# Weights split once and kept as parts in DRAM, the mixer's gates first, the output stage in idle buffers

## The chip, the cores and the metric

The kernel runs on one core of a Trainium2 chip. The metric is the device time of one execution in microseconds (us); lower is better. TensorE (PE) does the matmuls, VectorE (DVE), ScalarE (ACT) and GpSimd (POOL) the elementwise work, and every DMA is issued by SyncE (SP), whose queue works in order.

## The reference

One decoder block over 2048 tokens of width 1024, in float32:

```
h      = rmsnorm(x, norm_g) * (1 + scale) + shift        # scale, shift, gate from c @ w_ada + b_ada
q,k,v, z_attn, u, z_pool, g_attn, g_pool = split(h @ w_in)
attn   = three groups of dilated window attention, joined by a softmax over their log-denominators
y_attn = (attn * silu(z_attn)) @ w_attn_br
pooled = trailing mean of u over 2, 4, 8 or 16 tokens (one window a group of 128 channels), minus u
mixed  = pooled @ pool_w (per group) * pool_scale
y_pool = (mixed * silu(z_pool)) @ w_pool_br
merged = sigmoid(g_attn) * y_attn + sigmoid(g_pool) * y_pool
out    = rmsnorm(x + gate * (merged @ w_out), final_g)
```

## The kernel before

**Halves and products.** The tokens are worked in two halves of 1024 (h = 0, 1). Every large operand is held as two float32r parts, high and low; a product is three matmuls, high x high, high x low and low x high (`mm3`, L255: one k-step is six matmuls of 512 columns; one projection of 128 columns is eight k-steps into the PSUM tile `mm`).

**The weights.** They lie packed in DRAM as 80 blocks of 512 KB (`stream`, `pack_weights`). The stream `order` runs over all 80, then again over the last 8 (`w_out`, used once per quarter), and all that twice, so 176 blocks are fetched. `fetch_raw` (L203) loads a block into `wraw` (two buffers), and `fetch_part` splits a half block into the tiles `whi` (a DVE cast, L217) and `wlo` (a POOL subtraction, L218). There are six of each, so parts are made up to six ahead. A part's buffer is refilled two `tick`s after the k-step that read it last. Each `fetch_raw` is placed in SP's queue right behind the split that frees its buffer.

**The order of work.** PE and SP keep the order in which the program is written; DVE, ACT and POOL are ordered by a planner. Each half does twelve units (four head pairs, three groups each: `unit` projects k, q, v), while the attention of the unit before is woven in as a side queue. In a unit of the last group, `load_rows` (L639) fetches the other groups' results from DRAM, `output` joins them on DVE (L756 to L773), and `joined` transposes the result on PE (L777). Then come:

- `pool_in`: four projections of u, with the attention of the last unit woven in; after each, `pool_sums` queues the running sums of that group on DVE (L879 to L896);
- `pool_out`: four projections of z_pool, each followed by sigmoid, the group's small matmuls (L926) and a split into `gated`;
- `branch` (pool), `attn_gate`, `branch` (attention), where each of eight turns multiplies a gate's projection by a product with `gated`;
- `out_half` twice (quarters q = 0, 1): `merged @ w_out` (L1003, 32 steps of twelve 256-column matmuls), `finish` adds the product to `y` (rows of x loaded again, L276), and `normed` scales a row tile into a new tile `yo` and stores it.

In half 0, `ahead` and `next_h` run beside the two `out_half`s and prepare half 1: eight tiles of x are loaded (`new_x`, L276), normed (`x_norm`, L293 to L295), transposed on PE two tiles at a time (`transposed_x`, L340; eight steps a pair of tiles) and split into `hparts` (L345 to L348). In `next_h`, tiles 4 to 7 are loaded after the pass over a pair ends, and normed in steps 3 and 4 of the next pass.

**Buffers.** Most [128 x 1024] tiles come from one pool of `NBIG` = 33 slots (`b4`): `hparts` (16 slots), `gated`, `merged`, the splits of `merged`, x, `y`, `yo`, `yt`, and the two rows `gate` and `fg` among them. A tile waits for a slot to come free, and a DMA that waits for one holds SP's queue.

Of the kernel before, what the change touches and what calls it, by code (L numbers as in the profile page):

```python
# [11 lines left out]
F32 = mybir.dt.float32  # L12
# [134 lines left out]
def block_kernel(ctx: ExitStack, tc: tile.TileContext, x, cols, b_gate, w_ada, wpk, pool_w, rel_bias, final_g, onehot,  # L147
# [38 lines left out]
    def mm():  # L186
        return ps_mm.tile([P, HALF], F32, name="mm", tag="mm")
# [97 lines left out]
    def new_x(h, p):  # L285
        xt = b4(name="x")
        load_x(h, p, xt)
        return xt
# [540 lines left out]

    def branch(hparts, gated, merged, mparts=None):  # L830

# [3 lines left out]
        for u in range(4):  # L835
# [3 lines left out]
            for j in range(2):  # L839
                ps = mm()  # L840
                yield from mm3(ps, take("col"), hparts)
                sg = sigmoid(ps)
# [5 lines left out]
                ps = mm()  # L848
                yield from mm3(ps, wb, gated, slice(j * P, (j + 1) * P), frees=(j == 1))
                msl = slice(j * 512, j * 512 + 512)  # L850
# [10 lines left out]

    def pool_in(h, hparts, pooled, todo):

        for gi in range(4):
            ps = mm()
            for _ in mm3(ps, take("col"), hparts):
                next(todo[0], None) if todo else None
                yield
            cur = b4(name="u0")
            nc.scalar.copy(out=cur, in_=ps)  # L870
            todo[:] = [chain(*todo, pool_sums(h, gi, cur, pooled))]

    def pool_sums(h, gi, u0, pooled):
# [24 lines left out]
        phi, plo = b4(F32R, "phi"), b4(F32R, "plo")  # L898
        split(phi, plo, cur)
        pooled.append((phi, plo))  # L900
        yield

    def pool_weights():
# [5 lines left out]
        return pwh, pwl  # L909

    def pool_out(hparts, pooled, gated, pwh, pwl, todo):
        for gi in range(4):
            ps = mm()
            for _ in mm3(ps, take("col"), hparts):
                next(todo[0], None)
                yield
            assert len(pooled) > gi
            sg = sigmoid(ps)
            nc.vector.tensor_tensor(out=sg, in0=ps, in1=sg, op=ALU.mult)
            phi, plo = pooled[gi]  # L920
            gsl = slice(gi * P, (gi + 1) * P)
            for q in range(2):
                sl = slice(q * 512, (q + 1) * 512)
                ps = bank(q)
                for i, (w, m) in enumerate(((pwh, phi), (pwh, plo), (pwl, phi))):
                    nc.tensor.matmul(ps, lhsT=w[:, gsl], rhs=m[:, sl], start=(i == 0), stop=(i == 2))  # L926
                nc.vector.scalar_tensor_tensor(out=sg[:, sl], in0=ps, scalar=psc_col[:, gi:gi + 1], in1=sg[:, sl],
                                               op0=ALU.mult, op1=ALU.mult)
            ghi, glo = b4(F32R, "gphi"), b4(F32R, "gplo")
            split(ghi, glo, sg)  # L930
            gated.append((ghi, glo))

# [35 lines left out]
    def out_half(h, q, mparts, rows_bc):  # L968
# [16 lines left out]
        def normed(p):  # L985
            y = ys[p]
            ssq = sm.tile([P, 1], F32, name="ssq")
            nc.vector.tensor_reduce(out=ssq, in_=ssqs[p], axis=AX.X, op=ALU.add)
            r = rstd(ssq, nc.gpsimd)
            yo = b4(name="yo")  # L990
            nc.vector.tensor_tensor(out=yo, in0=y, in1=fg_bc, op=ALU.mult)
            nc.scalar.activation(out=yo, in_=yo, func=AF.Copy, scale=r)
            t0 = h * HALF + (4 * q + p) * P
            store(out[t0:t0 + P, :], yo, 2)

        for n in range(4):
# [9 lines left out]
            if n < 3:  # L1006

                for k in range(KC):
# [32 lines left out]
    for h in range(2):  # L1041
# [3 lines left out]
        for hp in range(4):  # L1045
            for g in GORDER:
# [12 lines left out]
                n_queue = 7 if g else 8  # L1059
        pooled, merged, gated = [], [], []  # L1060
        pwh, pwl = pool_weights()
        todo = []
        weave(pool_in(h, hparts, pooled, todo), 32, queue, n_queue, 1)
        run(queue)
# [8 lines left out]
        nc.sync.dma_start(out=rows_bc[1], in_=final_g.partition_broadcast(P))  # L1073
        mparts = []
# [61 lines left out]
```

## Time and profile before

| | |
|---|---|
| median of 3 runs | 2218.45 us (2213.07 to 2219.28) |
| profiled execution | 2212.21 us, of which the span from first to last instruction is 2210.2 us |
| PE busy | 2137.7 us (97% of the span) |
| DVE, ACT, POOL busy | 933.1, 597.6, 805.9 us |
| DMA | 198.48 MB, mean 90 GB/s |
| mean granted TensorE clock | 0.989 |

Busy times overlap; the engine with the longest is PE. A wait of PE is a stretch in which it had nothing running, put down to the instruction that ended it.

### The profile page before, as it was taken

The page shows a single profiled execution, that of the slowest core. Times are in us where ns is not written, and L with a number is a line of the kernel's source. Part 1 is how long each engine was busy: PE and PEld are TensorE (multiplying, and loading weights), DVE is VectorE, ACT ScalarE, POOL GpSimd, SP SyncE. Part 2 cuts the span into 40 slices and gives each one's busy share as a digit, 9 for nine tenths or more (in the row PEclk, how much of TensorE's full clock was granted, in tenths as well). Part 3 has the DMA queues.
Part 4 walks back from the last instruction along what each step waited for, and adds up shares of the span by engine and source line. Part 5 has one row for each costly group of instructions (what it writes and reads, how often), then busy time and mean ns, then how long its engine had stood idle before and what let it go on. Part 6 is the DMA issues. An engine that isn't in the chain of part 4 may idle for free.

```text
span 2210.2 us, 30824 instructions
## 1 busy us (share of the span) xinstructions
PE 2137.7 (97%) x11786; PEld 1808.5 (82%) x11786; DVE 933.1 (42%) x2144; ACT 597.6 (27%) x1487; POOL 805.9 (36%) x669
## 2 busy tenths in 40 slices
PE   6999999999999999999799999999999999999998
PEld 4888888888878888889778878888888788888898
DVE  6536335263382111117743464553644831111164
ACT  4423333233321001003433333333333310010023
POOL 3313222132243225437743232332333432253375
PEclk9999999999999999999999999999999999999999
DMA  8442232222211112114432333223222111121134
GB/s 294 142 153 73 81 95 73 73 74 80 76 60 42 48 48 87 52 43 172 162 120 87 89 90 89 72 82 111 81 81 86 53 48 48 48 86 48 48 134 162
DMA packets 142675, 198.48 MB, mean 90 GB/s; under 512 B 13542, under 2 KB 109983, under 8 KB 142528
## 3 DMA queue, kind: packets, MB, share of 16 engines
q1 hardware_dynamic: 142528, 196.51, 27.9%
q8 instruction: 93, 1.52, 0.3%
q14 instruction: 54, 0.44, 0.1%
HBM read 157.62 MB, written 35.16 MB: 87 GB/s over the span
## 4 chain that ended last, share of the span: by engine, by line
PE 42%; DVE 3%; DMA 2%; issue 2%; POOL 2%; ACT 1%; SPq 0%; POOLq 0%; DVEq 0%; ACTq 0%
PE mm L255 33%; PE mm L1003 3%; PE knot L738 3%; PE qk L682 2%; DMA row<-rows 1%; POOL wlo L218 1%; PE knot L717 1%; PE knot L646 1%; ACT l L692 1%; DMA wraw<-in_wpk_dram 1%; DVE wd L762 0%; DVE l L701 0%; DVE whi L217 0%; PE hp L926 0%; POOL y L982 0%
## 5 line engine op out<-in xcount | busy, mean ns | idle before, releaser
L218 POOL TENSOR_TENSOR wlo<-wraw,whi 128x512 fp32r<-128x512 f32 x352 | 476.4, 1357 | 995.9 <-DVE whi L217 549.6
L255 PE MATMUL mm<-hhi,whi 128*128 128x512 f32 x2000 | 637.8, 400 | 0.0
L255 PE MATMUL mm<-hlo,whi 128*128 128x512 f32 x2000 | 621.4, 392 | 0.0
L255 PE MATMUL mm<-hhi,wlo 128*128 128x512 f32 x2000 | 619.5, 391 | 0.0
L217 DVE CAST whi<-wraw 128x512 fp32r<-128x512 f32 x349 | 189.6, 547 | 754.0 <-PE mm L255 628.7
L255 PEld LDWEIGHTS mm<-hhi,wlo 128*128 128x128 f32 x2000 | 377.4, 189 | 81.8
L255 PEld LDWEIGHTS mm<-hlo,whi 128*128 128x128 f32 x2000 | 377.1, 189 | 81.4
L255 PEld LDWEIGHTS mm<-hhi,whi 128*128 128x128 f32 x2000 | 364.7, 189 | 72.0 <-issue 0.5
L820 ACT ACTIVATE sg<-mm 128x1024 f32<-128x1024 f32 x48 | 49.4, 1028 | 555.1 <-PE mm L255 443.2
L686 DVE CUSTOM_DVE_ANT_0 l<-qk,bias 128x256 f32<-128x256 f32 (+1 forms) x384 | 126.0, 384 | 129.2 <-PE qk L682 105.9
L692 ACT ACTIVATE l<-l,row 128x256 f32<-128x256 f32 (+1 forms) x256 | 117.2, 460 | 149.0 <-DVE row L686 126.7
L1003 PE MATMUL mm<-whi,mhi 128*128 128x256 f32 x512 | 149.2, 291 | 1.0 <-DVE yt L1032 0.7
L1003 PE MATMUL mm<-whi,mlo 128*128 128x256 f32 x512 | 146.2, 286 | 2.5 <-POOL mlo L827 2.5
L1003 PE MATMUL mm<-wlo,mhi 128*128 128x256 f32 x512 | 145.9, 285 | 0.0
L738 PE MATMUL knot<-v,pT 128*128 128x64 f32 x768 | 131.5, 270 | 3.2 <-ACT pT L727 2.9
L738 PEld LDWEIGHTS knot<-v,pT 128*128 128x128 f32 x768 | 112.7, 193 | 5.7 <-ACT pT L727 3.2
L702 POOL TENSOR_TENSOR l<-l,ident 128x512 f32<-128x512 f32 (+1 forms) x56 | 71.6, 1278 | 108.5 <-DVE l L701 97.7
L738 PE MATMUL knot<-vd,pT 128*128 128x64 f32 x560 | 109.6, 278 | 1.3 <-DVE wd L762 1.3
L1003 PEld LDWEIGHTS mm<-whi,mlo 128*128 128x128 f32 x512 | 99.2, 194 | 3.3 <-POOL mlo L827 3.3
L1003 PEld LDWEIGHTS mm<-whi,mhi 128*128 128x128 f32 x512 | 99.5, 194 | 1.9 <-DVE yt L1032 1.5
L1003 PEld LDWEIGHTS mm<-wlo,mhi 128*128 128x128 f32 x512 | 99.5, 194 | 0.1
L727 ACT COPY pT<-knot 128x512 f32<-128x512 f32 x96 | 56.4, 588 | 155.1 <-PE knot L738 67.7
(175 smaller groups left out, 2497.3 us busy)
## 6 DMA issues: line engine op xcount, KB each, us to landing
wraw<-in_wpk_dram SPq DMA_DIRECT2D x176, 512.0 KB, 3.7
rows<-row SPq DMA_DIRECT2D x128, 66.0 KB, 1.7
row<-rows SPq DMA_DIRECT2D x64, 132.0 KB, 3.4
wada<-in_w_ada_dram SPq DMA_DIRECT2D x32, 256.0 KB, 5.5
x<-in_x_dram SPq DMA_DIRECT2D x16, 512.0 KB, 6.3
y<-in_x_dram SPq DMA_DIRECT2D x16, 512.0 KB, 7.7
out_dram<-yo SPq DMA_DIRECT2D x16, 512.0 KB, 6.5
khist<-kh SPq DMA_DIRECT2D x52, 128.0 KB, 2.5
```

The costliest lines, as they stand in the source:

```text
L217: copy(out=hi, in_=raw)
L218: nc.gpsimd.tensor_tensor(out=lo, in0=raw, in1=hi.bitcast(F32), op=ALU.subtract)
L255: nc.tensor.matmul(ps[:, n * 512:(n + 1) * 512], lhsT=w, rhs=m[:, n * 512:(n + 1) * 512], start=(k == 0 and j == 0), stop=(k == nk - 1 and ...
L646: nc.tensor.transpose(ps[:, (t % 4) * P:(t % 4) * P + P], res["vT"][:, k0:k0 + P], ident)
L682: nc.tensor.matmul(qks[i][:, j * 256:j * 256 + nk], lhsT=qt[qi][a], rhs=keys[ki][a], start=(n == 0), stop=(n == 2))
L686: nc.vector.tensor_tensor_reduce(out=l[:, 2 * j + i, 256 - nk:], in0=qks[i][:, j * 256:j * 256 + nk], in1=bt[:, i, 256 - nk:], scale=-1.0, ...
L692: nc.scalar.activation(out=ll, in_=ll, func=AF.Exp, scale=-1.0, bias=nd[:, j, i:i + 1], accum_out=nd[:, j, 2 + i:3 + i])
L702: nc.gpsimd.tensor_tensor(out=prev, in0=prev, in1=ident.unsqueeze(1).broadcast_to([P, 4 - f, P]), op=ALU.mult)
L727: nc.scalar.copy(out=pT[:, 1], in_=pps)
L738: nc.tensor.matmul(ops[:, j, hs], lhsT=d["pT"][:, b, 2 * j + i, :], rhs=vv[:, hs], start=(b == 1), stop=(b == 0 or not full))
L820: nc.scalar.activation(out=s, in_=ps, func=AF.Sigmoid)
L1003: nc.tensor.matmul(pst[:, pos:pos + 256], lhsT=st, rhs=mv, start=(fresh and i == 0), stop=(last and i == 2))
```

## The change

1. **Parts in DRAM.** When a block is split for the first time, both parts of each half block are also stored to a DRAM tile `wsp` (three ticks later). From the second time on, a half block is two 256 KB loads into `whi` and `wlo`, with no cast, no subtraction and no `wraw`.
2. **Mixer's gates first.** `pool_gates` (the z_pool projections) now runs where `pool_in` ran, beside the last attention. `pool_mix` then projects u, the groups in the order 3, 2, 1, 0; each group's sums, small matmuls and split (`pool_group`) are advanced one step per k-step of the projections that follow, those of the first turn of `branch` included. In that turn, the product with `gated` takes the groups in the order 3 to 0. Group 0 does its two subtractions on DVE.
3. **Output stage.** `gate`, `fg` (in two halves) and `yt` move from the 33 slots into attention tiles that are idle then (`pT`, `bias`, `l`); `yo` is gone, `y` is scaled in place.
4. **next_h.** Tiles of x are loaded at step 3 of the pass over an earlier pair, and normed in steps 4 and 5 of the next pass.

```diff
-    seq += [("in", OFF_U + c * P, "col") for c in range(4)]
     seq += [("in", OFF_ZP + c * P, "col") for c in range(4)]
+    seq += [("in", OFF_U + c * P, "col") for c in range(3, -1, -1)]
...
+    wsp = dram.tile([n_blocks, 2, 2, P, 512], F32, name="wsp")
...
-        if i < len(order):
+        if i < n_blocks:
             t = b4(name="wraw") if i == 2 else wp.tile([P, HALF], F32, name="wraw", tag="wraw", bufs=2)
...
         b, q = divmod(i, 2)
+        if b >= n_blocks:
+            hi = wp.tile([P, 512], F32R, name="whi", tag="whi", bufs=6)
+            lo = wp.tile([P, 512], F32R, name="wlo", tag="wlo", bufs=6)
+            for j, t in enumerate((hi, lo)):
+                nc.sync.dma_start(out=t.bitcast(F32), in_=wsp[order[b], q, j])
+            parts[i] = (hi, lo)
+            state["part"] = i + 1
+            return
...
         nc.gpsimd.tensor_tensor(out=lo, in0=raw, in1=hi.bitcast(F32), op=ALU.subtract)
+        for j, t in enumerate((hi, lo)):
+            store(wsp[b, q, j], t.bitcast(F32), 3)
...
-                if p and p < 6 and i in (3, 4):
-                    x_norm(tiles[p + i - 1])
+                if p and p < 6 and i in (4, 5):
+                    x_norm(tiles[p + i - 2])
+                if p < 4 and i == 3:
+                    tiles += [new_x(1, p + 4), new_x(1, p + 5)]
                 yield
-            if p < 4:
-                tiles += [new_x(1, p + 4), new_x(1, p + 5)]
...
+                for _ in mm3(ps, take("col"), hparts):
+                    advance(todo)
+                    yield
+                run(*todo)
...
+                turn = -1 if todo and not (u or j) else 1
+                yield from mm3(ps, wb[::turn], gated[::turn], slice(j * P, (j + 1) * P), frees=(j == 1))
...
+    def pool_gates(hparts, sgs):
+        for gi in range(4):
+            ps = mm()
+            yield from mm3(ps, take("col"), hparts)
+            sg = sigmoid(ps)
+            nc.vector.tensor_tensor(out=sg, in0=ps, in1=sg, op=ALU.mult)
+            sgs.append(sg)
+    def pool_mix(h, hparts, sgs, gated, pwh, pwl, todo):
+        gated += [None] * 4
+        for gi in range(3, -1, -1):
+            ps = mm()
+            for _ in mm3(ps, take("col"), hparts):
+                advance(todo)
+                yield
+            cur = b4(name="u0")
+            nc.scalar.copy(out=cur, in_=ps)
+            todo.append(pool_group(h, gi, cur, sgs, gated, pwh, pwl))
+    def pool_group(h, gi, u0, sgs, gated, pwh, pwl):
+        pooled, n = [], 0
+        for _ in pool_sums(h, gi, u0, pooled):
+            n += 1
+            yield
+        for _ in range((7, 8, 10, 11)[gi] - n):
+            yield
...
+        split(ghi, glo, sg, nc.gpsimd if gi else nc.vector)
+        gated[gi] = ghi, glo
...
-            yo = b4(name="yo")
-            nc.vector.tensor_tensor(out=yo, in0=y, in1=fg_bc, op=ALU.mult)
-            nc.scalar.activation(out=yo, in_=yo, func=AF.Copy, scale=r)
+            for i in range(2):
+                sl = slice(i * 512, (i + 1) * 512)
+                nc.vector.tensor_tensor(out=y[:, sl], in0=y[:, sl], in1=fg_bc[i], op=ALU.mult)
+            nc.scalar.activation(out=y, in_=y, func=AF.Copy, scale=r)
...
-                t = b4(name="yt").rearrange("p (t c) -> p t c", c=256)
+                t = att.tile([P, 4, 256], F32, name="yt", tag="l", bufs=2)
...
-        weave(pool_in(h, hparts, pooled, todo), 32, queue, n_queue, 1)
+        weave(pool_gates(hparts, sgs), 32, queue, n_queue, 1)
         run(queue)
-        run(pool_out(hparts, pooled, gated, pwh, pwl, todo))
-        run(branch(hparts, gated, merged))
+        todo = []
+        run(pool_mix(h, hparts, sgs, gated, pwh, pwl, todo))
+        run(branch(hparts, gated, merged, todo=todo))
...
-        rows_bc = b4(name="gate"), b4(name="fg")
+        rows_bc = (att.tile([P, D], F32, name="gate", tag="pT", bufs=1),
+                   [att.tile([P, 512], F32, name="fg", tag="bias", bufs=2) for _ in range(2)])
```

## Rows read from the trace of the kernel before

**Rows 1.** The page: busy time, share of the span and instructions of each engine.

```profile
PE 2137.7 (97%) x11786; PEld 1808.5 (82%) x11786; DVE 933.1 (42%) x2144; ACT 597.6 (27%) x1487; POOL 805.9 (36%) x669
```

**Rows 2.** Windows: stretch, length, busy us per engine (xcount), granted clock, DMA share, GB/s.

```profile
600.00:650.00 50.00, 45.52 (x242) 37.83 (x241) 46.56 (x101) 15.21 (x41) 24.82 (x15) 0.93 0.12 40
700.00:800.00 100.00, 100.00 (x443) 82.81 (x442) 16.71 (x31) 6.20 (x7) 25.64 (x20) 1.00 0.15 48
1001.00:1048.00 47.00, 45.17 (x370) 44.36 (x369) 36.25 (x37) 14.28 (x37) 37.79 (x32) 1.00 0.52 182
1060.00:1072.00 12.00, 10.35 (x88) 10.14 (x88) 10.23 (x16) 5.23 (x9) 8.93 (x10) 1.00 0.97 380
1722.00:1756.00 34.00, 29.03 (x145) 24.65 (x144) 32.62 (x67) 10.51 (x25) 14.85 (x9) 0.90 0.14 46
```

**Rows 3.** PE's waits, 1040 to 1120 us: us in total, times, longest.

```profile
PE hp L340 <- DVE x L295: 16.6, 3, 8.0
PE hp L340 <- ACT hraw L345: 1.7, 1, 1.7
```

**Rows 4.** Chain of work that ended last, 1085 to 1120 us: start, us, what.

```profile
1093.53 2.56 PE mm L1003 x12
...
1099.71 0.22 PE knot L340 x2
1099.92 1.43 PE mm L1003 x12
...
1106.45 4.05 DMA x<-in_x_dram
```

**Rows 5.** SP's waits, 1040 to 1120 us.

```profile
SPq L276 <- PE knot L340: 19.7, 2, 15.9
SPq L276 <- ACT yt L983: 6.5, 2, 3.7
```

**Rows 6.** PE's waits by stretch, in the order 100:600, 1125:1720, 600:660, 1700:1760, 2100:2210.

```profile
PE knot L777 <- DVE row L773: 5.5, 3, 2.0
...
PE knot L777 <- DVE row L773: 7.0, 3, 3.6
...
PE knot L777 <- DVE row L773: 3.2, 3, 2.2
PE knot L738 <- DVE wd L762: 1.3, 1, 1.3
...
PE knot L738 <- ACT pT L727: 2.9, 1, 2.9
PE knot L777 <- DVE row L773: 2.1, 2, 1.7
...
PE mm L1003 <- POOL mlo L827: 1.3, 2, 1.0
```

**Rows 7.** Timeline, 1284 to 1295 us: start, us, engine line op names.

```profile
1284.75 0.42 DVE L217 CAST whi<-wraw 128x512 fp32r<-128x512 f32 x1
...
1286.29 1.60 POOL L218 TENSOR_TENSOR wlo<-wraw,whi 128x512 fp32r<-128x512 f32 x1
...
1287.92 0.34 SPq L203 DMA_DIRECT2D wraw<-in_wpk_dram  x1
...
1288.43 0.79 SPq L639 DMA_DIRECT2D row<-rows  x2
...
1293.92 0.17 DVE L756 TENSOR_REDUCE mn<-row 128x4 f32<-128x12 f32 x1 [2.94 <-DMA row<-rows]
```

**Rows 8.** The page, costliest groups: line, engine, names, xcount, busy us, mean ns.

```profile
L218 POOL TENSOR_TENSOR wlo<-wraw,whi 128x512 fp32r<-128x512 f32 x352 | 476.4, 1357 | 995.9 <-DVE whi L217 549.6
```

**Rows 9.** DMA issues: xcount, KB each, median us to landing.

```profile
wraw<-in_wpk_dram SPq DMA_DIRECT2D x176, 512.0 KB, 3.7
...
x<-in_x_dram SPq DMA_DIRECT2D x16, 512.0 KB, 6.3
...
bias<-btab SPq DMA_DIRECT2D x24, 256.0 KB, 3.0
```

More of the change, by code (lines that the diff above doesn't have):

```diff
@@ L828, in msplit, with branch @@
         return [(hi[:, j * 512:(j + 1) * 512], lo[:, j * 512:(j + 1) * 512]) for j in range(2)]
-    def branch(hparts, gated, merged, mparts=None):
+    def branch(hparts, gated, merged, mparts=None, todo=()):
         add = bool(merged)
@@ L840, in branch @@
                 ps = mm()
-                yield from mm3(ps, take("col"), hparts)
+                for _ in mm3(ps, take("col"), hparts):
+                    advance(todo)
+                    yield
+                run(*todo)
                 sg = sigmoid(ps)
@@ L848, in branch @@
                 ps = mm()
-                yield from mm3(ps, wb, gated, slice(j * P, (j + 1) * P), frees=(j == 1))
+                turn = -1 if todo and not (u or j) else 1
+                yield from mm3(ps, wb[::turn], gated[::turn], slice(j * P, (j + 1) * P), frees=(j == 1))
                 msl = slice(j * 512, j * 512 + 512)
@@ L860, in branch @@
             mparts += msplit(merged[0][3])
-    def pool_in(h, hparts, pooled, todo):
+    def pool_gates(hparts, sgs):
         for gi in range(4):
             ps = mm()
+            yield from mm3(ps, take("col"), hparts)
[6 more added lines that the diff above has]
+            ps = mm()
             for _ in mm3(ps, take("col"), hparts):
-                next(todo[0], None) if todo else None
+                advance(todo)
                 yield
@@ L870, in pool_in, with advance @@
             nc.scalar.copy(out=cur, in_=ps)
-            todo[:] = [chain(*todo, pool_sums(h, gi, cur, pooled))]
+            todo.append(pool_group(h, gi, cur, sgs, gated, pwh, pwl))
+    def advance(gens):
+        for i in gens:
+            next(i, None)
+    def pool_group(h, gi, u0, sgs, gated, pwh, pwl):
[5 more added lines that the diff above has]
+            yield
+        sg = sgs[gi]
+        phi, plo = pooled[0]
+        gsl = slice(gi * P, (gi + 1) * P)
+        for q in range(2):
+            sl = slice(q * 512, (q + 1) * 512)
+            ps = bank(q)
+            for i, (w, m) in enumerate(((pwh, phi), (pwh, plo), (pwl, phi))):
+                nc.tensor.matmul(ps, lhsT=w[:, gsl], rhs=m[:, sl], start=(i == 0), stop=(i == 2))
+            nc.vector.scalar_tensor_tensor(out=sg[:, sl], in0=ps, scalar=psc_col[:, gi:gi + 1], in1=sg[:, sl],
+                                           op0=ALU.mult, op1=ALU.mult)
+        ghi, glo = b4(F32R, "gphi"), b4(F32R, "gplo")
+        split(ghi, glo, sg, nc.gpsimd if gi else nc.vector)
+        gated[gi] = ghi, glo
     def pool_sums(h, gi, u0, pooled):
@@ L898, in pool_sums @@
         phi, plo = b4(F32R, "phi"), b4(F32R, "plo")
-        split(phi, plo, cur)
+        split(phi, plo, cur, nc.gpsimd if gi else nc.vector)
         pooled.append((phi, plo))
@@ L909, in pool_weights @@
         return pwh, pwl
[L911 to L931, printed above, removed]
     def attn_gate(h, hparts, gated):
@@ L989, in normed @@
             r = rstd(ssq, nc.gpsimd)
-            yo = b4(name="yo")
-            nc.vector.tensor_tensor(out=yo, in0=y, in1=fg_bc, op=ALU.mult)
-            nc.scalar.activation(out=yo, in_=yo, func=AF.Copy, scale=r)
+            for i in range(2):
+                sl = slice(i * 512, (i + 1) * 512)
+                nc.vector.tensor_tensor(out=y[:, sl], in0=y[:, sl], in1=fg_bc[i], op=ALU.mult)
+            nc.scalar.activation(out=y, in_=y, func=AF.Copy, scale=r)
             t0 = h * HALF + (4 * q + p) * P
-            store(out[t0:t0 + P, :], yo, 2)
+            store(out[t0:t0 + P, :], y, 2)
         for n in range(4):
@@ L1059, in block_kernel @@
                 n_queue = 7 if g else 8
-        pooled, merged, gated = [], [], []
+        merged, gated, sgs = [], [], []
         pwh, pwl = pool_weights()
+        weave(pool_gates(hparts, sgs), 32, queue, n_queue, 1)
+        run(queue)
         todo = []
-        weave(pool_in(h, hparts, pooled, todo), 32, queue, n_queue, 1)
-        run(queue)
-        run(pool_out(hparts, pooled, gated, pwh, pwl, todo))
-        run(branch(hparts, gated, merged))
+        run(pool_mix(h, hparts, sgs, gated, pwh, pwl, todo))
+        run(branch(hparts, gated, merged, todo=todo))
         gated = []
@@ L1070, in block_kernel @@
         run(branch(hparts, gated, merged, m0))
-        rows_bc = b4(name="gate"), b4(name="fg")
+        rows_bc = (att.tile([P, D], F32, name="gate", tag="pT", bufs=1),
+                   [att.tile([P, 512], F32, name="fg", tag="bias", bufs=2) for _ in range(2)])
         nc.sync.dma_start(out=rows_bc[0], in_=gate_d)
-        nc.sync.dma_start(out=rows_bc[1], in_=final_g.partition_broadcast(P))
+        for i in range(2):
+            nc.sync.dma_start(out=rows_bc[1][i], in_=final_g[i * 512:(i + 1) * 512].partition_broadcast(P))
         mparts = []
```

## The prediction

> **What bounds the kernel now.** I read the page first: PE is busy for 97% of the span [rows 1]. In the windows the middle of a half has PE busy 100.00 of 100.00 us with 443 matmuls of 512 columns, one every 226 ns, at a granted clock of 1.00 [rows 2]. The change takes no matmul away, so nothing can be won there: all it can give back is PE's waits and the slow clock after them. The span holds about 72 us without a matmul (2210.2 - 2137.7), and PE's waits by stretch say where those lie that the change can reach: the end of half 0, the joins of the attention units, the change from attention to pooling, and a little in the first `out_half` of half 1 [rows 3, 6]. The chain and SP's waits then say what is late in each. The sum is a sum over those places.
>
> **Half 0's last quarter.** Between 1040 and 1120 us PE waits 16.6 us for normed tiles of x and 1.7 us for `hraw` [rows 3]. After such a wait, twelve matmuls that otherwise take 1.43 us take 2.56 us: the clock stands at the lower of its two levels, 1.2 instead of 2.4 GHz [rows 4]. That is 1.1 us for the twelve and some more before and after them, 1.5 us by my estimate, twice. In all some 21 us. What is late: SP waited 19.7 us in two waits for a transposed tile's slot and 6.5 us for a slot of `yt`, with the load of x at the head of its queue [rows 5]; the last tile was loaded at 1106.45 and PE needed it at about 1108 [rows 4]. Counting slots in the second pass: 16 of `hparts`, 8 of the split `merged`, 4 of `y`, 2 rows, 1 `yt` are 31 of 33, which leaves two for x, where tiles 2 and 3 are still being transposed; tiles 4 and 5 have no place. After the change the rows and `yt` are elsewhere: 28 are taken, five are left for x, so tiles 2, 3, 4, 5 and one more fit. A step of this stage takes 1.43 + 0.22 = 1.65 us [rows 4]. A load now comes nine steps (15 us) ahead of its norm instead of four (6.6 us), against 6.3 us to landing [rows 9]. Only tile 7 lacks a slot until step 15, when tiles 2 and 3 are done; its norm is at step 21, still 10 us on. On the other side, `y` itself is now held until its store has landed, and the seventh and eighth pair of `hparts` need those slots: I leave 4 us of waits for that. Gain 17 us; bounds 5 (the slots are short again) and 21.
>
> **The joins of half 1.** In the units of half 1 PE waits three times for the joined rows, 7.0 us in all [rows 6]. The longest one in the timeline: the cast `whi` is issued at 1284.75, `wlo` waits for POOL and ends at 1287.89, and only then SP issues the next `wraw` and behind it, at 1288.43, the two loads of rows, which land at 1293.9, behind 512 KB of weights [rows 7]. After the change there is no `wlo` and no `wraw` in half 1: the fetch waits for PE alone, which had released the cast, so the loads of rows go out about 3 us earlier, behind 0.8 us for issuing two part loads. I take 6 of the 7.0 us, and one stretch of low clock after the longest wait (about 1.5 us, as above) with it: 7 us; bounds 2 and 8.5.
>
> **From attention to pooling.** Half 0 waits 3.2 + 1.3 = 4.5 us there, half 1 2.9 + 2.1 = 5.0 us [rows 6], and the windows show why: DVE is busy 46.56 of 50 us and 32.62 of 34 us, because the running sums compete with the last attention [rows 2]. The granted clock in them is 0.93 and 0.90 [rows 2], which takes 0.07 x 50 = 3.5 us and 0.10 x 34 = 3.4 us at most, part of it while PE waits anyway: 2.5 us each. So 14.5 us. `pool_gates` leaves DVE four products there instead of the sums; the sums get 44 us of projections and the first 11 us of `branch` for themselves. What stays is the join that other units have, about 2 us a half. What is late next: group 0's `gated`. Its small matmuls end the projection; a DVE product, an ACT copy and a DVE subtraction follow, some 3.5 us by the like instructions (0.7, 1.0, 1.2 and the hand-overs), and PE reaches it as the fourth k-step, 3 x 6 x 0.226 = 4.1 us later. It fits by half a microsecond; I put 0.5 us a half on it (bounds 0 and 4, if DVE has something else in front). Gain 9 us; bounds 3 and 14.
>
> **In the first quarter of half 1** PE waits 1.3 us for POOL's `mlo`, which shares POOL with `wlo` [rows 6]; with 192 subtractions of 1357 ns less in the stream [rows 8], it goes: 1 us.
>
> **What is added.** 160 half blocks give 320 stores of 256 KB, all but the last few in half 0, and from then on 384 loads of 256 KB replace 96 of 512 KB: some 84 MB written and 50 MB more read. In the attention of half 0 they come between the loads of rows in SP's order. Two stores ahead of a load of rows cost it two issues (0.8 us, as the two in [rows 7]) and the time of 512 KB at the 380 GB/s that a window reached [rows 2], 1.4 us. The joins there wait 5.5 us already [rows 6]; those at the head now are behind a `wraw`, not where the stores come, so I take 2 us of loss (bounds 0 and 9: four joins by 2.2 us). The three-tick delay means a store never waits for its data. In the first quarter of half 0 the traffic is 47 us x 182 GB/s = 8.6 MB [rows 2]; ten half blocks are stored (5.2 MB) and six more are already loaded as parts (3.1 MB), less five `wraw` (2.6 MB): 14.3 MB in 47 us is 304 GB/s, below the 380 GB/s of the window at 1060 [rows 2]. It is hidden, with 80% of the queue full: loss 1 us, bounds 0 and 5. The store in place and the two halves of `fg` change nothing that PE waits for; after the last matmul the same DVE and ACT work remains.
>
> One limit is less clear. A 512 KB weight load lands in 3.7 us, a 256 KB one (`bias`) in 3.0 us [rows 9], so halving a DMA saves little of its time; that several run at once is seen only from the 380 GB/s, 2.7 times what one 512 KB load reaches by itself. The Trainium skill (DMA: Bandwidth & Descriptors, Anatomy of one DMA and Bandwidth) has the same shape: 2.0 us fixed plus the bytes, and the advice to make DMAs of 1 MiB or more. By its figures a part's two loads would take 5.2 us one after the other, 2.3 us more than PE's 2.9 us with a part of `w_out`, or 37 us a quarter; no run so far shows 256 KB loads queued like that. Where they did not is a rival below.
>
> **The sum.** 17 + 7 + 9 + 1 - 2 - 1 = 31 us off the profiled execution's 2212.2 us: 2181 us. The runs' median lies 6.2 us above the profiled execution; with that, 2187 us.
>
> **The rivals.**
>
> *The last quarter keeps its waits.* With `y` held until it lands and six tiles of x wanted at once, the slots are short again, and SP stands at a load of x as before (15.9 us, [rows 5]). Now no `wraw` is ahead: behind SP's wait stand the part loads, five parts of two steps (3.3 us) ahead, 16.5 us less 3 to 5 us of landing. A 15.9 us wait then costs PE 3 to 5 us for weights besides, so of the 17 us some 3 to 5 remain. Against it: three slots are really freed. Time: 2187 + 13 = 2200 us.
>
> *Half 0 pays.* Stores and rows collide at every join, with the clock falling after each (9 + 4 x 1.5 = 15 us), and the joins of half 1 keep half their waits (3 us). Together with the forecast's other terms 2187 + 16 = 2203 us; if the first rival comes too, 2216 us, no change. For it: the joins wait for loads of rows that land late now [rows 7].
>
> *Slower: part loads do not overlap enough.* In `out_half` PE uses a part in 24 matmuls of 256 columns, 2 x 1.43 = 2.9 us [rows 4]. Two loads of 3.0 us each, one after the other, are 6.0 us: PE would wait 3.1 us for each of 16 parts, 50 us a quarter, in three quarters: 2187 + 150 = 2337 us. The point from which it decides is 6.0/2.9 = 2.1 loads at once; at 1.5 at once it is 1.1 x 48 = 53 us, so 2240 us. Against it: the 2.7 above.
>
> *Nothing to be had*, since the planner orders DVE, ACT and POOL anew and other waits open: within 6.7 us of 2218.
>
> **How the numbers follow.** Forecast 0.60 (its own range 2174 to 2200 us), first rival 0.13, half 0 pays 0.12 (a quarter of it no change), nothing to be had 0.08, slower by the parts or by new waits 0.07. A difference under 0.3% (6.7 us) can't be told from none in this kernel. Faster: 0.60 + 0.13 + 0.09 = 0.82; same 0.11; slower 0.07. The range goes from the forecast with all gains at their upper bounds, 21 + 8.5 + 14 + 1 = 44 us less than 2218, to the joint second rival: 2174 down to 2170 for what the joins of half 0 may give, up to 2212 us.
>
> **What would show it.** Right: no `wlo` after the first quarter of half 0; PE's wait for x in the last quarter under 5 us and the clock there near 1; the L777 waits of half 1 under 2 us; DVE in the window of `pool_gates` well under 90%. Wrong: SP waiting for slots at L276 as long as now; PE waiting at L255 or L1003 for DMAs of `wsp`, a wait that the trace of before does not have; the L777 waits of half 0 over 8 us; a new wait at the first turn of `branch` for group 0's split.

## The result, and the profile after

The changed kernel takes 2164.27 us (median of 4 runs, 2162.96 to 2165.88) against 2217.9 us (4 runs, 2213.07 to 2219.28): a ratio of 0.9762, 95% interval 0.9745 to 0.9779, faster. The forecast was 2187 us; the measured time lies 5.7 us below the lower end of the range, 2170 us. The profiled execution took 2164.82 us with a span of 2163.0 us, 47.4 us less than the one of before.

The page shows PE still as the bound, with 14 us less busy time (the same matmuls at a mean granted clock of 0.996 instead of 0.989), and POOL and DVE relieved [rows 1]. Below it are the costliest group that answers to [rows 8], and the DMA issues that answer to [rows 9]:

```profile
PE 2123.8 (98%) x11786; PEld 1798.5 (83%) x11786; DVE 800.1 (37%) x1972; ACT 611.9 (28%) x1499; POOL 533.3 (25%) x473
...
L228 POOL TENSOR_TENSOR wlo<-wraw,whi 128x512 fp32r<-128x512 f32 x160 | 216.3, 1355 | 555.0 <-DVE whi L227 274.7
...
whi<-wsp SPq DMA_DIRECT2D x192, 256.0 KB, 2.7
wlo<-wsp SPq DMA_DIRECT2D x192, 256.0 KB, 2.8
wraw<-in_wpk_dram SPq DMA_DIRECT2D x80, 512.0 KB, 4.4
```

Windows of the changed kernel, with the columns of [rows 2]: attention to pooling of half 0, the first quarter of half 0, its last quarter, attention to pooling of half 1, and a stretch of the last quarter of half 1.

```profile
600.00:650.00 50.00, 50.00 (x271) 42.55 (x270) 31.51 (x84) 19.17 (x39) 14.01 (x13) 1.00 0.42 143
...
989.00:1042.00 53.00, 48.82 (x385) 47.90 (x384) 36.71 (x44) 17.47 (x44) 35.80 (x34) 0.97 0.80 291
1042.00:1096.00 54.00, 53.64 (x451) 53.05 (x451) 36.44 (x74) 30.98 (x71) 26.69 (x40) 1.00 0.77 278
...
1717.00:1751.00 34.00, 34.00 (x152) 28.15 (x151) 18.13 (x27) 8.10 (x8) 9.64 (x5) 1.00 0.28 93
2108.00:2122.00 14.00, 12.76 (x105) 12.39 (x104) 1.98 (x3) 3.17 (x10) 3.77 (x6) 1.00 1.00 389
```

PE's waits that are left, for the stretches 100 to 600, 670 to 990, 990 to 1036, 1036 to 1130 and 2060 to 2215 us; between 600 and 670 and between 1125 and 1770 us there is none (L789 is the L777 of before, L1035 is L1003, L919 is L926):

```profile
PE knot L789 <- DVE row L785: 1.8, 1, 1.8
...
PE hp L919 <- POOL plo L257: 2.5, 1, 2.5
...
PE mm L1035 <- DVE whi L227: 1.8, 1, 1.8
PE mm L1035 <- POOL mlo L839: 1.3, 2, 1.0
PE mm L1035 <- POOL wlo L228: 1.1, 1, 1.1
...
PE mm L1035 <- DMA wlo<-wsp: 0.2, 1, 0.2
...
PE mm L1035 <- DMA whi<-wsp: 1.1, 1, 1.1
PE mm L1035 <- DMA wlo<-wsp: 0.4, 2, 0.2
```

Against [rows 3, 6] the waits of the last quarter (but 0.2 us), of the change to pooling and of half 1's joins are gone; two of the three joins of half 0 too. New are one wait for group 1's `plo`, those for `whi` and `wlo` in the first quarter, and three for parts at the end of half 1. The 1.3 us for `mlo` in the first quarter of half 0 are not new: the kernel before has the same row there.

Where the time went, by stage: the times between landmarks of PE (the last `qk`, the first matmul of each output quarter, the last transpose), worked out from the traces, one execution each. Runs e1 to e15 are explained below.

| stage, us | before | after | e1 parts | e2 gates | e3 output | e7 parts + output | e8 | e9 | e10 |
|---|---|---|---|---|---|---|---|---|---|
| units, half 0 | 611.1 | 603.7 | 603.9 | 610.2 | 615.4 | 608.2 | 602.2 | 605.8 | 601.4 |
| pooling, branches | 389.8 | 385.9 | 390.4 | 385.9 | 391.6 | 390.0 | 385.9 | 385.9 | 382.9 |
| first quarter | 49.2 | 52.8 | 50.3 | 49.3 | 54.3 | 52.3 | 52.4 | 55.6 | 53.4 |
| last quarter | 75.2 | 53.8 | 70.1 | 75.7 | 69.0 | 53.1 | 57.7 | 70.5 | 53.1 |
| units, half 1 | 592.1 | 582.6 | 582.6 | 591.0 | 590.8 | 582.6 | 582.6 | 582.6 | 582.6 |
| pooling, branches | 390.3 | 381.5 | 381.5 | 383.8 | 390.4 | 381.5 | 381.5 | 381.5 | 381.5 |
| first quarter | 48.5 | 46.1 | 46.1 | 48.1 | 49.9 | 46.1 | 46.1 | 46.1 | 46.1 |
| last quarter, tail | 54.1 | 56.7 | 55.8 | 54.1 | 55.9 | 56.3 | 56.7 | 56.2 | 54.5 |
| span | 2210.2 | 2163.0 | 2180.8 | 2198.0 | 2217.3 | 2170.0 | 2164.9 | 2184.1 | 2155.4 |

A stage is known less well than its last digit says. The change profiled once more (e12) differs by 1.2 us at most. Where joins wait it can be more: e7 has e1's program up to the output stage, and its units of half 0 took 608.2 us instead of 603.9, where two of its waits are each followed by 3.4 us at the lower clock.

### The profile page after: what moved, and what is told of

It is laid out like the page before. It is cut to its first block, busy times and chain, and to the rows that moved or that the text cites. A ratio compares the mean times of both kernels' runs of the same rounds, so it can differ in the third digit from the quotient of the medians.

```text
span 2163.0 us, 31345 instructions
## 1 busy us (share of the span) xinstructions
PE 2123.8 (98%) x11786; PEld 1798.5 (83%) x11786; DVE 800.1 (37%) x1972; ACT 611.9 (28%) x1499; POOL 533.3 (25%) x473
## 4 chain that ended last, share of the span: by engine, by line
PE 91%; DMA 4%; issue 2%; POOL 1%; DVE 1%; SPq 1%; ACT 1%; POOLq 0%; DVEq 0%; ACTq 0%
PE mm L267 71%; PE knot L750 6%; PE mm L1035 4%; PE qk L694 4%; PE knot L729 2%; PE knot L658 1%; PE mm L502 1%; DMA x<-in_x_dram 1%; DMA wada<-in_w_ada_dram 1%; DMA whi<-wsp 1%; DMA wlo<-wsp 1%; PE hp L919 1%; PE vp L502 0%; DMA row<-rows 0%; POOL wlo L228 0%
## 5 line engine op out<-in xcount | busy, mean ns | idle before, releaser
L228 POOL TENSOR_TENSOR wlo<-wraw,whi 128x512 fp32r<-128x512 f32 x160 | 216.3, 1355 | 555.0 <-DVE whi L227 274.7
L227 DVE CAST whi<-wraw 128x512 fp32r<-128x512 f32 x157 | 83.0, 534 | 364.3 <-PE mm L267 293.3
L832 ACT ACTIVATE sg<-mm 128x1024 f32<-128x1024 f32 x48 | 49.3, 1028 | 494.9 <-PE mm L267 442.1
L1035 PE MATMUL mm<-whi,mhi 128*128 128x256 f32 x512 | 148.2, 289 | 2.9 <-DVE whi L227 1.8
L1035 PE MATMUL mm<-wlo,mhi 128*128 128x256 f32 x512 | 146.0, 285 | 1.7 <-POOL wlo L228 1.1
L1035 PE MATMUL mm<-whi,mlo 128*128 128x256 f32 x512 | 145.6, 284 | 1.3 <-POOL mlo L839 1.3
L1035 PEld LDWEIGHTS mm<-whi,mhi 128*128 128x128 f32 x512 | 98.7, 193 | 3.5 <-DVE whi L227 2.1
L1035 PEld LDWEIGHTS mm<-wlo,mhi 128*128 128x128 f32 x512 | 98.9, 193 | 2.6 <-POOL wlo L228 1.3
L1035 PEld LDWEIGHTS mm<-whi,mlo 128*128 128x128 f32 x512 | 98.8, 193 | 1.7 <-POOL mlo L839 1.7
```

The lines of the kernel that those rows point to most:

```text
L832: nc.scalar.activation(out=s, in_=ps, func=AF.Sigmoid)
L1035: nc.tensor.matmul(pst[:, pos:pos + 256], lhsT=st, rhs=mv, start=(fresh and i == 0), stop=(last and i == 2))
```

## Experiments

### One part at a time (e1 to e4)

e1 is the kernel before with the diff's hunks of `stream`'s parts alone (`wsp`, the stores, the loads of parts); e2 with the mixer's gates first alone; e3 with the output stage and the new times in `next_h`; e4 only stores the parts and reads none:

```diff
+        if b < n_blocks:
+            for j, t in enumerate((hi, lo)):
+                store(wsp[b, q, j], t.bitcast(F32), 3)
```

> Only part 1 (parts stored to DRAM and loaded again). If each part of the change pays in its own place: the joins of half 1 lose their waits (9 us) and the joins of half 0 theirs (7 us, as in the changed kernel), the pooling stages and the last quarter of half 0 keep most of theirs (15 and 15 to 21 us); about 15 to 20 us faster than before. If the gain lay in the slots and in DVE's load alone: under 9 us.

> Only part 2 (the mixer's gates first). If each part pays in its own place: the L777 and L738 waits at the end of both halves' attention fall from 4.5 and 5.0 us to about 2, with the clock staying up: 8 to 13 us faster, joins of the other units as before. If those waits were POOL's and SP's (weights split there) and not DVE's: under 4 us.

> Only parts 3 and 4 (output stage in idle tiles, x loaded earlier). If the slots were what was late: PE's wait for x in the last quarter of half 0 falls from 16.6 us to under 5, 12 to 21 us faster. If SP stands behind wlo there anyway, so that earlier loads don't go out earlier without part 1: half of the wait stays, 5 to 11 us.

> Only the stores of part 1: 320 stores of 256 KB more, the second passes still load and split. As the forecast had it (the stores collide with the loads of rows): 0 to 9 us slower, the L777 waits of half 0 at or above 5.5 us. If the stores change the order in which DVE and POOL are planned, and the 7 us won at the joins of half 0 come from that: those waits fall to about 2 us, and the kernel is 3 to 8 us faster though it only does more.

Measured, against 2214.62 us: e1 2184.68 us (0.9867, 0.9853 to 0.9882); e2 2200.19 us (0.994, 0.9926 to 0.9955); e3 2215.95 us (1.0008, 0.9999 to 1.0018); e4 2209.24 us (0.9982, 0.9968 to 0.9996). The parts alone gain 29.9 us, more than either theory allowed, and the gates 14.4. The output stage alone gives nothing, which misses both of its theories: the 6.2 us of the last quarter are there, but the first quarter is 5.1 us longer. Stores alone, which only add work, do not make the kernel slower. The first three do not add up to the change, and the table shows why at two places.

The last quarter of half 0 gains 5.1 us in e1, 6.2 in e3 and 21.4 in the change. SP's waits there, 1036 to 1130 us, first e3, then e1, with one row of PE's waits in e1:

```profile
SPq L203 <- POOL wlo L218: 57.6, 9, 13.9
SPq L203 <- POOL ms L280: 14.1, 2, 13.8
SPq L276 <- PE knot L340: 4.6, 3, 3.9
```

```profile
SPq L288 <- PE knot L352: 23.0, 2, 15.9
SPq L220 <- PE mm L1015: 18.0, 2, 13.0
...
PE mm L1015 <- DMA whi<-wsp: 4.7, 1, 4.7
```

With the slots free (e3), SP hardly waits for one (4.6 instead of 19.7 us, [rows 5]), but now longer for POOL ahead of `wraw`, and the loads of x are late behind that: PE waits 6.8 us for x. This could be seen before: the longest row of the view behind [rows 5], 1040 to 1120 us of the kernel before, is not among its rows:

```profile
SPq L203 <- POOL wlo L218: 27.0, 5, 13.3
```

With the parts alone (e1), SP stands at a load of x for 15.9 us as before, and PE's wait for a part, 4.7 us, comes on top: the first rival's price (3 to 5 us).

The other way round, half 1's change to pooling gains 6.5 us in e2, 8.8 us in e1 and 8.8 us in the change: the gates alone give three quarters, and the parts alone all of it. In half 0 only the gates give it (385.9; e1 390.4).

### Both parts of the last quarter, its load times and its slots (e7, e8, e9)

e7 is e1 with e3. e8 is the changed kernel with the hunk in `next_h` undone, e9 is e8 with the two rows back in the 33 slots:

```diff
-        rows_bc = (att.tile([P, D], F32, name="gate", tag="pT", bufs=1),
-                   [att.tile([P, 512], F32, name="fg", tag="bias", bufs=2) for _ in range(2)])
+        fg = b4(name="fg")
+        rows_bc = b4(name="gate"), [fg[:, :512], fg[:, 512:]]
```

> The parts in DRAM together with the output stage and the new times of the loads of x, without the mixer's gates first. Theory 1 (in the last quarter of half 0 the free slots and the end of wlo at the head of SP's queue are needed together): the last quarter takes 53 to 57 us, as with the whole change (53.8), and the time is that of the whole change plus the 13 us of the gates, 2175 to 2180 us. Rival (the two parts add up: 5.1 us by the parts alone and 6.2 us by the output stage alone): the last quarter takes 63 to 66 us, the time is 2184 to 2188 us.

> The changed kernel, with the tiles of x loaded and normed in the last quarter of half 0 when they were before (loaded when a pass ends, normed in steps 3 and 4 of the next). The slots are freed, the parts come from DRAM. Theory 1 (both are needed: a load that ends four steps, 6.6 us, ahead of its norm is late against 6.3 us to landing and the parts beside it): PE waits 4 to 10 us for x there, the last quarter takes 60 to 66 us, the time is 2170 to 2177 us. Rival (the free slots do it all): the last quarter stays at 53 to 56 us and the time within 3 us of 2164.

> The changed kernel with the old times of the loads of x in the last quarter of half 0 (as in the run before this one that took 57.7 us there and 2168 us in all), and gate and fg back in two of the 33 slots; yt and the scaled y stay as the change has them. Theory 1 (slots are what the loads of x wait for): two slots fewer bring PE's wait for x back to 8 us or more with its slow clock, the last quarter takes 64 to 70 us, the time is 2174 to 2182 us. Rival (with SP free of wlo, three slots are enough): the last quarter stays at 56 to 60 us, the time within 3 us of 2168.

Measured: e7 2169.88 us (0.9803, 0.9786 to 0.9819), e8 2167.72 us (0.9795, 0.9778 to 0.9813), e9 2183.8 us (0.9859, 0.9842 to 0.9877). e7's last quarter takes 53.1 us: the two parts are needed together. Its span is only 7.0 us over the change's, so its time is under what its theory gave: 4.1 us in the pooling of half 0, 4.5 us in half 0's units (the low clock named above; the gates come later), and nothing in half 1, where the gates' worth was the parts' already. e8 lies between its two theories: PE waits once, 3.2 us, for x, and the quarter takes 3.9 us more than with the change. e9, with two slots fewer than e8, takes 12.8 us more there and shows the slots as the cause: SP's wait for one and PE's waits in the last quarter, for x and, as in e1, for parts:

```profile
SPq L288 <- PE knot L352: 23.3, 2, 14.9
...
PE hp L352 <- DVE x L307: 6.2, 1, 6.2
PE mm L1035 <- DMA whi<-wsp: 4.7, 2, 4.2
PE mm L1035 <- DMA wlo<-wsp: 2.1, 2, 1.2
```

Gate and fg in slots together with the new load times was not tried.

### The joins (e5, e6, e13, e14)

A tick is one k-step of PE. e5 is the kernel before with each weight block's load moved three ticks behind the split. e6 is e4 with stores of one row; e13 and e14 are e4 with the stores one and five ticks after the split:

```diff
# e5, with a line in tick() that calls fetch_raw() when an entry of late runs out
-            fetch_raw()
+            late.append(3)
# e6
+                store(wsp[b, q, j][0:1, :], t[0:1, :].bitcast(F32), 3)
# e13 (0: issued at the next tick), e14 (5); a line in tick() issues them
+                kept.append([0, wsp[b, q, j], t.bitcast(F32)])
```

> The kernel before, with one thing moved: the load of the next weight block is issued three ticks after the split that frees its buffer, not right behind it. Nothing else changes, and no part is kept. Theory 1 (the loads of rows for a join are late because SP stands in front of them waiting for the subtraction wlo): the waits for joined rows, 5.5 us in half 0 and 7.0 us in half 1, fall to under 3 us together, the stretches of low clock after them go, and the time falls by 8 to 13 us, to about 2204 us. Rival (the joins are late because of the order of DVE's own work): the waits stay between 9 and 14 us together and the time within 4 us of before.

> The kernel before with the 320 stores of parts, each cut from 128 rows to one row of 2 KB, and nothing read back. The run with the full stores had units of half 0 that took 603.8 us instead of 611.1 and a time of 2209 us. Theory 1 (the planner orders DVE and POOL otherwise when the stores are there, and their traffic costs nothing): units of half 0 at 603 to 605 us here too, time 2206 to 2211 us. Rival A (the traffic does cost, and the order gains more than was seen): units of half 0 at 601 us or less, time at least 2 us under the full stores. Rival B (the gain needs the full stores): units of half 0 back at 610 to 612 us, time 2214 us.

> The kernel before with the 320 full stores alone, each issued one tick after its split and not three. Theory 1 (a store makes its part due in SP's order, so the planner makes the part earlier; the sooner the store, the sooner the part): SP's wait for wlo ahead of the weight loads between 100 and 600 us falls further, from 169.8 us with three ticks (296.7 without stores) to 150 us or less; joined rows wait under 2 us there. Rival (that there are stores matters, not when): 165 to 175 us, as with three ticks. Second rival (SP, now standing for the stores themselves, sends the rows later): joined rows wait 3 us or more.

> The kernel before with the 320 full stores alone, each issued five ticks after its split. Theory 1 (the part is made by when its store is due): SP's wait for wlo ahead of the weight loads between 100 and 600 us lies between that with three ticks and that without stores, at 200 us or more, and joined rows wait 2 to 5 us there. Rival (that there are stores matters, not when): 165 to 175 us, joined rows under 2 us.

Measured, the first two against 2212.91 us, the others against 2213.58: e5 2200.49 us (0.9939, 0.9922 to 0.9955), e6 2206.42 us (0.9971, 0.9957 to 0.9986), e13 2214.49 us (1.0009, 1.0 to 1.0019), e14 2214.84 us (1.0006, 0.9995 to 1.0017).

e5 shows what the joins of the units wait for: with nothing but these loads moved out of SP's way, every join wait from 100 to 600 and from 1125 to 1690 us is gone, the units take 602.6 and 583.0 us, and the time falls by 0.61%. So in both halves the rows were late because SP stood at `wraw` for `wlo`. e5 also takes the block's 512 KB from in front of the rows, but these are not what counts: in e6 `wraw` is still issued right ahead of the rows (at 198.13 and 198.57 us at the first join), and its joins wait 0.2 us.

In half 0 the change keeps `wlo` and `wraw`; what moved is when `wlo` is made ahead of a join. The subtraction that SP stands for at the first join, in the kernel before, with stores after one (e13), three (e4) and five ticks (e14):

```profile
199.28 1.60 POOL L218 TENSOR_TENSOR wlo<-wraw,whi 128x512 fp32r<-128x512 f32 x1
```

```profile
198.90 1.29 POOL L225 TENSOR_TENSOR wlo<-wraw,whi 128x512 fp32r<-128x512 f32 x1
```

```profile
197.32 1.28 POOL L219 TENSOR_TENSOR wlo<-wraw,whi 128x512 fp32r<-128x512 f32 x1
```

```profile
198.73 1.28 POOL L225 TENSOR_TENSOR wlo<-wraw,whi 128x512 fp32r<-128x512 f32 x1
```

With stores after three ticks it ends 2.3 us sooner than before, with one and five 0.7 and 0.9 us sooner. It is not so elsewhere: of the 33 weight blocks loaded from 100 to 600 us, four go out more than 0.5 us sooner in e4 than before, counted by PE's matmuls, and three of these stand ahead of a join.

The expectations go by SP's total wait for `wlo` ahead of these loads, in the same order of runs:

```profile
SPq L203 <- POOL wlo L218: 296.7, 33, 16.2
```

```profile
SPq L210 <- POOL wlo L225: 168.9, 33, 8.3
```

```profile
SPq L204 <- POOL wlo L219: 169.8, 33, 8.6
```

```profile
SPq L210 <- POOL wlo L225: 234.5, 33, 13.2
```

This total misleads. A wait counts from SP's instruction before, so it shrinks when SP stands for the same parts at a store instead (36.6 us for `whi` and 26.5 us for `wlo` in e4). e13 and e14 differ by 66 us in it and by 0.2 us in when the subtraction above ends. Against theory 1 of e13, a sooner store makes no sooner part: with one tick `wlo` comes later than with three. Why the planner brings `wlo` forward at the joins when the stores are there stays open.

e13 and e14 gain nothing in all. One difference shows in the timeline of SP at this join, e4 first and then e13:

```profile
198.63 0.33 SPq L204 DMA_DIRECT2D wraw<-in_wpk_dram  x1
199.07 0.84 SPq L643 DMA_DIRECT2D row<-rows  x2
199.96 0.42 SPq L180 DMA_DIRECT2D wsp<-whi  x1
200.43 0.43 SPq L180 DMA_DIRECT2D wsp<-wlo  x1
```

```profile
200.22 0.33 SPq L210 DMA_DIRECT2D wraw<-in_wpk_dram  x1
200.59 0.43 SPq L179 DMA_DIRECT2D wsp<-whi  x1
201.07 0.43 SPq L179 DMA_DIRECT2D wsp<-wlo  x1
201.61 1.06 SPq L649 DMA_DIRECT2D row<-rows  x2
```

With three ticks the stores stand behind the rows, with one and with five two of them stand ahead, at all three joins from 100 to 600 us. So the rows are late twice over, by the later `wlo` and by the stores, and joins wait 4.0 and 4.4 us instead of 1.7 (5.5 before).

e6 has the three-tick order with 2 KB instead of 256 KB a store: joins wait 0.2 us, the units take 601.8 us. It fits neither of its theories in full. What the bytes cost shows best in half 0's change to pooling, 600 to 670 us, where two stores stand ahead of rows in both runs; PE's waits there, e4 first and then e6:

```profile
PE knot L781 <- DVE row L777: 6.4, 4, 3.2
```

```profile
PE knot L781 <- DVE row L777: 3.0, 3, 2.3
```

The kernel before has 3.2 us [rows 6]. So full stores ahead of rows do make a join late; with 2.0 us from the units, e6 reaches the first quarter 4.5 us sooner than e4. In the whole time it is 2.4 us by the two ratios, whose intervals overlap.

### More of the same on top of the change (e10, e11, e12, e15)

e11 moves the weight block's load three ticks back in half 0's attention. e10 adds three more edits, for the waits listed above; e15 is e10 with all four `mlo` on DVE again and the cast of w_out's blocks on ACT; e12 is the change itself.

```diff
-    split(phi, plo, cur, nc.gpsimd if gi else nc.vector)
+    split(phi, plo, cur, nc.gpsimd if gi > 1 else nc.vector)
...
-    mparts.extend(msplit(merged[1][i], nc.vector))
+    mparts.extend(msplit(merged[1][i], nc.vector if h or i % 2 else nc.gpsimd))   # e10
...
+                    if h * q and n == 0 and k % 2:
+                        load_x(h, 4 * q + k // 2, ys[k // 2])
...
+        if b >= first_out:      # e15
+            copy = nc.scalar.copy
```

> The changed kernel with four things added, each for a wait that its trace still shows. The weight block's load comes three ticks after the split in the attention of half 0 (the join at 474 us, 2.0 us); group 1's plo goes to DVE (2.7 us at 679 us, with 1.7 us of low clock behind it); in half 0 the last mlo of the first quarter goes to DVE and two of the four mlo of the second to POOL (0.4, 1.2, 2.0 and 1.3 us, with 1.7 us of low clock); in half 1 the loads of y in the last quarter are spread over its first eight steps (1.2, 0.4 and 0.4 us). Theory 1 (these waits come where the engine or the queue named is busy with something else): 8 to 13 us less than the changed kernel, 2151 to 2157 us, and the stages units of half 0, pooling of half 0, first quarter of half 0 and last quarter of half 1 shorter by 2, 4, 5 and 2 us. Rival (the planner orders anew and as many waits open elsewhere): within 3 us of the changed kernel.

> The changed kernel with only the first of those four: the weight block's load three ticks after the split in the attention of half 0. Theory 1 (in half 0 the joins wait for loads of rows that stand behind the subtraction wlo in SP's order, whatever the stores do): no wait of 0.5 us or more for joined rows between 100 and 670 us, the units of half 0 at 600 to 602 us, 1 to 4 us less in all than the changed kernel. Rival (the stores in SP's order make them late): the wait at 474 us stays at 1.5 us or more, the time is that of the changed kernel.

> The changed kernel itself, beside the others on the same chip, so that they can be compared with it: 2161 to 2168 us, 0.974 to 0.980 of before.

> The changed kernel with the four additions of the earlier run, but in the first quarter of half 0 the four mlo stay on DVE and the cast whi of the blocks of w_out goes to ACT, which is busy 17.5 of 53 us there. Theory 1 (PE waits there for whi because DVE has four mlo in front of it, 4.6 us in a row): the waits for whi and wlo (3.7 and 1.1 us in the earlier run) fall under 1 us together, the first quarter takes 47 to 50 us instead of 53.4, the time is 3 to 6 us under the earlier run's 0.9748 of before: 0.972 to 0.9735. Rival (ACT makes whi late as well, behind its four mhi casts of 1.0 us): the quarter stays at 52 us or more, the time within 0.1% of the earlier run.

Measured, the first three against 2215.96 us: e10 2159.61 us (0.9748, 0.973 to 0.9765), e11 2162.21 us (0.9761, 0.9743 to 0.9778), e12 2165.61 us (0.9776, 0.9759 to 0.9794); e15 2156.15 us (0.9746, 0.9733 to 0.976, against 2213.58). e11's units of half 0 take 601.8 us, and no join waits. e10's runs (2157.22 to 2161.55) all lie under e12's (2165.13 to 2167.16): it beats both kernels, by 6.0 us on the change, less than the 8 to 13 expected. Three edits worked: the join, the pooling (382.9 us; PE waits 1.1 us for DVE's `plo`), and the loads of `y`, since the waits for parts in the last quarter of half 1 are gone. The fourth did not: the first quarter takes 53.4 us. The `mlo` of the second quarter there, first e10, POOL's two and DVE's two, then the change, 1023.5 to 1029 us, with mean ns as the last number before the idle time:

```profile
1016.62 5.63 POOL L847 TENSOR_TENSOR mlo<-mg,mhi 128x1024 fp32r<-128x1024 f32 x2
...
1019.94 3.39 DVE L847 TENSOR_TENSOR mlo<-mg,mhi 128x1024 fp32r<-128x1024 f32 x1
...
1023.25 1.21 DVE L847 TENSOR_TENSOR mlo<-mg,mhi 128x1024 fp32r<-128x1024 f32 x1
```

```profile
L839 DVE TENSOR_TENSOR mlo<-mg,mhi 128x1024 fp32r<-128x1024 f32 x4 | 4.6, 1211 | 0.0
```

Two `mlo` on DVE take as long as four did: the first ends only 1.1 us after POOL's two have, the second, with POOL idle, takes 1.21 us. e15, without that, takes 51.0 us there, between its theories, and its time can't be told from e10's.

## Why the prediction was right or wrong

The forecast summed 31 us of gain for the profiled execution; 47.4 us were measured. By its steps:

- **Half 0's last quarter**, 17 us: measured 21.4. The slots and the load times were the mechanism (e8, e9). What the step did not see is that freeing the slots alone would have left x behind SP's wait for `wlo` (e3); the size holds because the parts took that wait away. The 4 us left for waits did not occur; 0.2 us did.
- **Joins of half 1**, 7 us: measured 9.5. The mechanism is the one that was put forward, as e5 shows with no part stored; the size was low.
- **From attention to pooling**, 9 us: measured 3.9 + 8.8 = 12.7. In half 0 it is the gates, and the 2 us a half that the step left for a join did not stay. In half 1 it credited the gates with what the parts give without them. DVE's load, which the step named, still fits as the cause: from 1702 to 1736 us of e1, the same place in the work, DVE is busy 25.99 us instead of 32.62 [rows 2], and PE all 34.00. The parts take more from DVE than casts. POOL is busy 9.23 us instead of 14.85, and small products of the join that in part had run beside POOL's work are shorter, first before, then e1:

```profile
L762 DVE TENSOR_TENSOR wd<-e,row 128x12 f32<-128x12 f32 x3 | 4.7, 1580 | 0.5 <-ACT e L760 0.5
```

```profile
L774 DVE TENSOR_TENSOR wd<-e,row 128x12 f32<-128x12 f32 x3 | 1.1, 379 | 0.5 <-ACT e L772 0.5
```

SP's queue is not enough to explain it: e5 moves SP's load out of the way and leaves the sums where they were, and PE still waits 4.5 us in that change to pooling (5.0 before). e2, which takes the sums away and leaves SP's queue as it was, ends these waits in both halves. No run changes DVE's load and nothing else.

Group 0's split made no wait. What came next was group 1's `plo`, third in POOL's queue behind `wlo` and `gplo` (2.5 us and a stretch of low clock); with it on DVE (e10) the stage took 3.0 us less.

- **First quarter of half 1**, 1 us: measured 2.4. The forecast left out what the part loads cost at the other end of half 1: in its last quarter they queue behind four loads of `y` at 389 GB/s and a DMA share of 1.00, and the quarter with its tail takes 2.6 us more (2.2 of it gone in e10). Not all of it need be the loads of parts: e3, without any, takes 1.8 us more there.
- **First quarter of half 0**, 1 us of loss: measured 3.6, inside its bounds, but not by DMA: PE waits for no transfer there. New are its waits for `whi` and `wlo`, 2.9 us, with four `mlo` in front of the cast on DVE, and 3.4 us at the lower clock. Stores alone lengthen this quarter by 2.6 us already, with 256 KB each (e4) and with 2 KB (e6) alike, so it is an order and not traffic. Why the planner orders it so stays open.
- **Joins of half 0**, 2 us of loss: measured 7.4 us of gain. This is the step that failed most. It priced stores that stand ahead of the rows in SP's order, and took DVE's and POOL's order as given. In fact the stores stand behind the rows at three ticks, and with them the `wlo` that SP stood for at a join ends some 2 us sooner. Stores ahead of the rows do cost, as the step said (e13 against e4; e4 against e6 in the change to pooling), but even so the joins of the units wait less than before (4.0 instead of 5.5 us). One premise was wrong besides: that a store after three ticks never waits for its data. From 100 to 600 us of the change SP stands 62 us at stores for parts:

```profile
SPq L180 <- DVE whi L227: 35.7, 20, 3.2
SPq L180 <- POOL wlo L228: 26.0, 25, 1.2
```

The gain is larger than the 3.7 us of waits that went, because with each of two of them went 3.4 us at half the clock, 1.7 us of work. Its size is known to some 4 us (e7's units gain 2.9).

- **The 6.2 us** between the profiled execution and the median, added to the sum: the change's profiled execution lies 0.6 us over its median, and over the 9 to 21 runs of before in the later comparisons the median was 0.7 to 3.8 us over 2212.2. A single median of three, out of runs that spread from 2208.5 to 2220.7 us, was taken for a property of the kernel. These 6.2 us and the 9.4 us of the step before are most of the 23 us between 2187 and 2164.

Of the rivals, part loads that do not overlap did not come: 384 loads of 256 KB, at 2.7 us each, cost PE 1.7 us in all. The forecast said that no run so far showed 256 KB loads queued, and this was wrong: the kernel before issues 24 such loads in a row at its start, and the window over them has 395 GB/s:

```profile
16.71 20.05 SPq L376 DMA_DIRECT2D wada<-in_w_ada_dram  x24
...
17.00:37.00 20.00, 14.81 (x74) 11.41 (x73) 17.66 (x24) 11.94 (x21) 11.06 (x15) 1.00 1.06 395
```

The Trainium skill (DMA: Bandwidth & Descriptors, Anatomy of one DMA) gives one DMA a fixed 2.0 us plus its bytes, fitted on DMAs issued from GpSimd; these are issued from SP. The trace agrees for 256 KB in the changed kernel (2.7 us; an estimate by that fit is 2.6) and lies above it for 512 KB (4.4 us; 3.2). It shows too that the fixed part is no charge on the queue, since loads of 256 KB came at 395 GB/s.

## What to carry to other kernels

Where one queue issues all loads, read what it stands for at the moment a late load is issued, not what the load fetches: here weight loads waiting for a subtraction held the rows, and with the slots free x as well, and moving those loads by three ticks gave a quarter of this change (e5). Where engines are ordered by a planner, an edit that only adds work can move the order of the rest, so it has no sign until it has run; and the same edit's place in the queue, a tick or two, can take the gain away again. A total of one queue's waits does not say when the thing waited for was made: look at one instance in the timeline. Two edits aimed at one stage are worth testing alone and together: in the last quarter each alone gave about a quarter of what both gave, in half 1's pooling one alone gave all and the other three quarters.

## What the runs showed that was not expected

DVE and POOL hold each other up. In e10 three 128x512 products on DVE took 1.78, 1.78 and 2.89 us beside POOL's subtractions and 0.69 us where POOL was idle, and of two like 128x1024 subtractions the first took 3.39 us and the second, with POOL idle, 1.21. The Trainium skill (SBUF — State Buffer, Who interferes with whom) gives the rule: a VectorE instruction with two SBUF inputs contends with a GpSimd instruction that reads SBUF, since its second input comes through the read port that the two share, and that port is an exclusive lock. The trace agrees: each of the slow ones ends 0.5 to 1.1 us after the POOL instruction that it met. It makes moving an operation from one to the other worth little where both are busy. It also reaches the critical path: of the three `wd` products shown above for the kernel before, one took 2.35 us beside a `plo` of 2.40 us on POOL.
